# A decoder block on one core: the tensor work of GpSimd moved to the vector engine

## The chip, the cores and the metric

The kernel runs on one core of a Trainium2 chip. The metric is the device time of one execution in microseconds. The median of three runs of the kernel before is 4898.55 us (4892.66 to 4910.54).

## The reference

One layer of a hybrid model for 512 tokens of width 2048, all in float32:

```python
def reference(x, mem, w_in, ..., ln_w, ln_b):
    h = hybrid_mixer(x, ...)                       # mLSTM heads and forgetting attention, gated, merged
    x = layer_norm(DN_ALPHA * x + h, ln_w[l, 0], ln_b[l, 0])
    h = memory_cross_attention(x, mem, ...)        # 256 memory rows
    x = layer_norm(DN_ALPHA * x + h, ln_w[l, 1], ln_b[l, 1])
    h = peer_ffn(x, peer_wq, peer_sub_keys, peer_u, peer_v)
    x = layer_norm(DN_ALPHA * x + h, ln_w[l, 2], ln_b[l, 2])

def peer_ffn(x, w_pq, sub_keys, expert_u, expert_v):
    q = (x @ w_pq).reshape(B, S, 8, 2, 128)
    sc = einsum('bshpd,hpnd->bshpn', q, sub_keys)
    top_s, top_i = lax.top_k(sc, 16)
    cand_s = top_s[..., 0, :, None] + top_s[..., 1, None, :]      # 16 x 16 sums
    best_s, best_pos = lax.top_k(cand_s.reshape(..., 256), 16)
    idx = ...                                      # the expert (of 16384) behind each best sum
    g = jax.nn.softmax(best_s, -1)
    a = einsum('tkd,td->tk', expert_u[idx], x)
    return einsum('tk,tkd->td', gelu(a) * g, expert_v[idx])
```

## The kernel before

**Products in two parts.** TensorE multiplies in a rounded format. To keep float32 accuracy every operand is split: the high part is a copy into the rounded format (ScalarE, L134), the low part is the operand less the high part (a subtraction of a 128x1024 tile, L137 on the vector engine, L136 on GpSimd). Each product is three matmuls: high by high, high by low, low by high. The matmuls with low weights come after those with high ones (`products`, L208).

**Weights** stream from HBM as tiles of 128x1024 (512 KB), in the order of use, loaded by SyncE's queue (`load_raw`, L148) into small rings: `raw`, `whi` and `wlo` have one to three buffers each. A raw buffer can be loaded again when both parts have been made from it. There are 1472 such tiles. Every `SHARE`-th, that is every eighth of those that `load_w` loads up to the end of the choice, has its low part made by GpSimd; during the first 16 tiles of the first mLSTM it is every third. 123 low parts are GpSimd's, 1349 the vector engine's.

**Stages.** The tokens are cut into block A (128) and B (384). First comes A's mixer, with the products of the memory woven into it, up to about 900 us. Then A's merge, cross attention and the query of its experts, woven with B's mLSTM. From about 1460 us, A's experts are gathered row by row (`gathered`): GpSimd issues an indirect load of 128 rows of 2048 (L905), the vector engine multiplies and sums each (L933, L936). Each gather waits for the low part that the vector engine was last given (`work["last"]`), which paces it. Meanwhile B's mixer, cross attention and query run up to about 3080 us. Of B's tokens 96 are gathered too, in two jobs of 64 and 32, and 288 are computed densely over all 16384 experts: `stage_a` (products with `uT`, from 2970 us), and `stage_o` (products with `vq`, from about 3660 us). `stage_o` needs the weights of the choice, which are spread out by one-hot products (L1256, L1262, L1264, about 3360 to 3660 us), written to HBM and read back. 76 chunks of `stage_a` are placed ahead of the first `stage_o`; a chunk is two weight tiles.

**The choice** (`select`) runs for two heads of one block of 128 tokens: top 16 of 128 four times, the 16 x 16 sums `cand` on GpSimd (L832), top 16 of those twice, then for each half of the index a comparison with a counter (L846, vector engine), a product with the indices on GpSimd (L847) and a sum (L848, vector engine). It is called 16 times: four times for A at 1345 to 1500 us, 12 times for B at about 3000 to 3350 us.

**The last norm** (`fin`) is called six times: once for A, once for each of the two gathered parts of B, three times at the very end for the dense tokens. Its first half of 1024 columns takes two vector instructions (L987, L988), its second half one of ScalarE (L990), one product of GpSimd (L991) and one sum of the vector engine (L992).

**Order.** A scheduler lays out each engine's instructions at build time from its own cost estimates, with what the code says as dependences; at run time each engine takes its list in order. GpSimd's list also has the gathers and most of the small transfers to and from HBM.

Of the kernel before, what the change touches and what calls it, by code (L numbers as in the profile page):

```python
# [10 lines left out]
F32 = mybir.dt.float32  # L11
# [4 lines left out]
AF = mybir.ActivationFunctionType  # L16
ALU = mybir.AluOpType
# [14 lines left out]
NDENSE = 288  # L32
GATHERED = ((64, 64), (32, 32))
GB = 48
SHARE = 8
NEG = -1.0e30
ALPHA = 2.0 ** 0.25
EPS = 1e-5
# [8 lines left out]
def build(tc, I, out):  # L47
    nc = tc.nc
    with ExitStack() as ctx:
# [25 lines left out]
        def nm(s):  # L75
            cnt[0] += 1
            return f"{s}_{cnt[0]}"
# [52 lines left out]
        nc.vector.tensor_copy(iota, ioti)  # L130


        def split(hi, lo, src, pool=False):
            nc.scalar.copy(hi, src)  # L134
            if pool:
                return nc.gpsimd.tensor_sub(lo, src, hi.bitcast(F32))  # L136
            return nc.vector.tensor_sub(lo, src, hi.bitcast(F32))  # L137

        def load_split(hi, lo, src):
# [4 lines left out]
        def load_raw(src, n=1024):  # L144
            rings.append(rings.pop(0))
            ring = rings[-1]
            raw = ring["pool"].tile([P, n], F32, tag="raw", bufs=ring["raw"], name=nm("raw"))
            nc.sync.dma_start(raw, src)  # L148
            return raw


        work = {"jobs": None, "rate": 0.0, "due": 0.0, "n": 0, "share": 0, "last": None, "hold": False,
                "quiet": 0, "normed": None}

        def load_pair(src, pool=False):

            raw = load_raw(src)
            ring = rings[-1]
            hi = ring["pool"].tile([P, 1024], F32R, tag="whi", bufs=ring["hi"], name=nm("whi"))
            lo = ring["pool"].tile([P, 1024], F32R, tag="wlo", bufs=ring["lo"], name=nm("wlo"))  # L160
            return hi, lo, split(hi, lo, raw, pool)


        mids = []
# [13 lines left out]
                ride()  # L178

        def load_w(src):  # L180
            work["n"] += 1
            pool = work["share"] and work["n"] % work["share"] == 0
            hi, lo, i = load_pair(src, pool)
            if not pool:
                work["last"] = i
            if work["quiet"]:

                work["quiet"] -= 1
                work["last"] = work["normed"]
            if work["jobs"] is not None and not work["hold"]:  # L190
                work["due"] += work["rate"]
                while work["due"] >= 1 and work["jobs"] is not None:
                    work["due"] -= 1
                    if next(work["jobs"], None) is None:
                        work["jobs"] = None
            return hi, lo
# [52 lines left out]
        def rstd(o, var, t):  # L249

            v, w = t
            nc.vector.tensor_scalar(v, var, EPS, None, op0=ALU.add)
            nc.scalar.activation(w, v, AF.Sqrt)
            nc.vector.reciprocal(w, w)
            nc.vector.tensor_mul(v, v, w)
            nc.vector.tensor_mul(v, v, w)
            nc.vector.tensor_scalar(v, v, -0.5, 1.5, op0=ALU.mult, op1=ALU.add)
            nc.vector.tensor_mul(o, v, w)
# [13 lines left out]
        for kt in range(8):  # L272
            raw = load_raw(I["xT"][kt])
# [8 lines left out]
        def gt(n):  # L282
            return gp.tile([36, S], F32, tag=n, name="g_" + n)

        z, a, e, u, F, gi, M, m = (gt(n) for n in ("z", "a", "e", "u", "F", "gi", "M", "m"))
# [532 lines left out]
        def select(tp, sel, h0, sc, bufs=2):  # L818

            def w(tag, shape, dt=F32):  # L820
                return tp.tile([P] + list(shape), dt, tag=tag, bufs=bufs, name=nm(tag))

            v, ix = w("v", [4, 16]), w("ix", [4, 16], U32)
            for j in range(4):
                top16(tp, sc[:, j * P:(j + 1) * P], P, v[:, j], ix[:, j], bufs)
            ixf = w("ixf", [4, 16])
            nc.vector.tensor_copy(ixf, ix)
            cand = w("cand", [2, 16, 16])
            vv = v.rearrange("p (h q) k -> p h q k", q=2)
            ii = ixf.rearrange("p (h q) k -> p h q k", q=2)  # L830
            full = [P, 2, 16, 16]
            nc.gpsimd.tensor_tensor(cand, vv[:, :, 0].unsqueeze(3).to_broadcast(full),  # L832
                                    vv[:, :, 1].unsqueeze(2).to_broadcast(full), op=ALU.add)
            b, pos = w("b", [2, 16]), w("pos", [2, 16], U32)
            for j in range(2):
                top16(tp, cand[:, j].rearrange("p a b -> p (a b)"), 256, b[:, j], pos[:, j], bufs)
            pi = w("pi", [2, 2, 16], U32)
            nc.vector.tensor_scalar(pi[:, 0], pos, 4, None, op0=ALU.logical_shift_right)
            nc.vector.tensor_scalar(pi[:, 1], pos, 15, None, op0=ALU.bitwise_and)
            pf = w("pf", [2, 2, 16])  # L840
            nc.vector.tensor_copy(pf, pi)
            it = iota[:, 0:16].unsqueeze(1).unsqueeze(1).to_broadcast(full)
            sl = slice(h0 * 16, h0 * 16 + 32)
            for q, m in ((0, "i0"), (1, "i1")):
                eq = w("eq", [2, 16, 16])
                nc.vector.tensor_tensor(eq, pf[:, q].unsqueeze(3).to_broadcast(full), it, op=ALU.is_equal)  # L846
                nc.gpsimd.tensor_mul(eq, eq, ii[:, :, q].unsqueeze(2).to_broadcast(full))  # L847
                nc.vector.tensor_reduce(out=sel[m][:, sl].rearrange("p (h k) -> p h k", h=2), in_=eq,  # L848
                                        axis=AX.X, op=ALU.add)

            nc.vector.tensor_tensor(sel["g"][:, sl].rearrange("p (h k) -> p h k", h=2), b,
                                    b[:, :, 0:1].to_broadcast([P, 2, 16]), op=ALU.subtract)
# [125 lines left out]
        def fin(row, i, acc, lw, n=P):  # L978
            st = fst.pop(i)[:n]
            nc.vector.bn_aggr(st[:, 24:26], st[:, 0:24])  # L980
            rstd(st[:, 26:27], st[:, 25:26], (st[:, 28:29], st[:, 29:30]))
            nc.vector.scalar_tensor_tensor(st[:, 27:28], st[:, 24:25], -1.0, st[:, 26:27], op0=ALU.mult, op1=ALU.mult)
            for q in range(2):
                sl = slice(q * 1024, (q + 1) * 1024)
                a = acc[:n, sl]
                if q == 0:
                    nc.vector.scalar_tensor_tensor(a, a, st[:, 24:25], lw[0][:n, sl], op0=ALU.subtract, op1=ALU.mult)  # L987
                    nc.vector.scalar_tensor_tensor(a, a, st[:, 26:27], lw[1][:n, sl], op0=ALU.mult, op1=ALU.add)  # L988
                else:
                    nc.scalar.activation(a, a, AF.Identity, scale=st[:, 26:27], bias=st[:, 27:28])  # L990
                    nc.gpsimd.tensor_mul(a, a, lw[0][:n, sl])  # L991
                    nc.vector.tensor_add(a, a, lw[1][:n, sl])  # L992
                nc.sync.dma_start(out[row:row + n, sl], a)

        def run(gen):
# [15 lines left out]


        A, B = Path(0, 1, XA), Path(1, 3, XB)
        work["share"] = SHARE
        with tc.tile_pool(name="sa", bufs=1, side="right", reuse_waits="tile") as sa:
            def aq(n=P):
                return sa.tile([P, P], F32, tag="q", bufs=10, name=nm("aq"))
# [25 lines left out]

            with tc.tile_pool(name="a1", bufs=1, side="right", reuse_waits="tile") as a1:
                first = mlstm(A, a1, dict(ka=1, pre=2, qk=6, v=2, o=2, nM=1, pt=2), hold_h)
                work["share"] = 3
                for _ in range(16):
                    next(first)
                work["share"] = SHARE
                pt = sm_bank()  # L1050
                for tb in range(TB):
                    for w, src in enumerate((gi, m)):
                        o = (w * TB + tb) * 4
                        nc.tensor.transpose(pt[:, o:o + 4], src[s4, tb * P:(tb + 1) * P], ident[s4, 32:36])
                nc.vector.tensor_copy(cols.rearrange("p a b c -> p (a b c)"), pt[:, :32])
                gts.close()
                with tc.tile_pool(name="mem", bufs=1, reuse_waits="tile") as mp:
                    mem = memory(mp)
                    weave(chain(first, branch_ml(A, HA, aq)), mem, 0.34)
                    run(mem)  # L1060
                    settle()
# [143 lines left out]
        with tc.tile_pool(name="topk", bufs=1, reuse_waits="tile") as tp:  # L1205
# [22 lines left out]
            for t in range(1, TB - 1):  # L1228
                for g in range(4):
                    select(tp, sel[t], 2 * g, scs[t, g])  # L1230
                soften(tp, sel[t]["g"])
        work["share"] = 0

        def o_bank(i=0):
            return BK["pool"].tile([P, 512], F32, tag="mm", bufs=BK["mm"], name=nm("po"))
# [6 lines left out]
        for hb in range(NDENSE // GB):  # L1242
            while turned * P < (hb + 1) * GB:
                bank = o_bank()
                n = min(P, NDENSE - turned * P)
# [6 lines left out]
            for q in range(GB // 4):  # L1252
# [6 lines left out]
                for u in range(4):  # L1259
# [3 lines left out]
                                            op0=ALU.is_equal, op1=ALU.mult)  # L1263
# [68 lines left out]
        jobs = chain(*(gathered(TB - 1, r0, n, 1 + i, lambda: work["last"], 1) for i, (r0, n) in enumerate(GATHERED)))  # L1332
# [146 lines left out]
```

## Time and profile before

| | |
|---|---|
| median of three runs | 4898.55 us |
| profiled execution | 4901.6 us |
| its span | 4899.9 us |
| mean granted clock of TensorE | 0.985 |
| TensorE busy | 4707.2 us (96%) |
| vector engine busy | 3736.8 us (76%) |
| ScalarE busy | 2130.8 us (43%) |
| GpSimd busy | 1345.5 us (27%) |
| HBM traffic over the span | 292 GB/s |

In the views, PE is TensorE's matmuls and PEld its weight loads, DVE the vector engine, ACT ScalarE, POOL GpSimd, and SP SyncE. A group's row gives line, engine, operation, output and inputs, shapes, and count; behind the first bar busy us and mean ns of one, behind the second the idle time just before and what ended it. A row of waits gives who waited for whom: us in total, times, longest. A busy TensorE is not one at its peak, since matmuls overlap.

### The profile page before, as it was taken

The numbers are of one execution on the slowest core, as the hardware profiler recorded it, in microseconds if no ns is written. First come the engines' busy times: TensorE is split into PE (matmuls) and PEld (weight loads), VectorE is DVE, ScalarE is ACT, GpSimd is POOL, SyncE is SP. The second block draws the span as 40 slices with busy tenths as digits, with TensorE's granted clock in tenths as the row PEclk, the third lists the DMA queues.
The fourth block names the chain that finished last, engine by engine and source line by source line (L and its number), as shares of the span: only waits on it lengthen the run. The fifth ranks groups of instructions, "written<-read, shape, count | busy, mean of one in ns | idle before, by whom it ended". The sixth has DMA issues, their size and how long they took to land. (4 is left out here: it accounts for less than half of the span.)

```text
span 4899.9 us, 75254 instructions
## 1 busy us (share of the span) xinstructions
PE 4707.2 (96%) x28705; PEld 4347.4 (89%) x28705; DVE 3736.8 (76%) x5360; ACT 2130.8 (43%) x3108; POOL 1345.5 (27%) x1058
## 2 busy tenths in 40 slices
PE   7999999999999899999989999999998999999997
PEld 6888778878888899999988779999998999999997
DVE  7776666765698776887768585899877878888886
ACT  6665666555643322343332334434443433343333
POOL 2122222311124444434444232231111222221111
PEclk9999999999999999999999999999999999999999
DMA  7888888866559898998889584588788989989994
GB/s 259 277 290 281 290 321 311 281 226 200 193 188 357 332 358 338 342 334 328 301 297 381 192 298 164 205 281 281 282 290 325 347 339 350 345 332 348 359 336 146
DMA packets 380026, 1433.60 MB, mean 293 GB/s; under 512 B 43852, under 2 KB 104908, under 8 KB 320624
## 3 DMA queue, kind: packets, MB, share of 16 engines
q1 hardware_dynamic: 266208, 831.34, 47.9%
q0 software_dynamic: 91712, 559.45, 30.4%
q10 hardware_dynamic: 21744, 38.02, 2.1%
q8 instruction: 224, 3.67, 0.3%
q14 instruction: 138, 1.13, 0.1%
HBM read 1339.13 MB, written 89.40 MB: 292 GB/s over the span
## 5 line engine op out<-in xcount | busy, mean ns | idle before, releaser
L134 ACT CAST whi<-raw 128x1024 fp32r<-128x1024 f32 x1472 | 1526.1, 1051 | 1769.0 <-PE mm L208 780.0
L137 DVE TENSOR_TENSOR wlo<-raw,whi 128x1024 fp32r<-128x1024 f32 x1349 | 1690.3, 1265 | 711.5 <-ACT whi L134 496.2
L905 POOL DMA_INDIRECT rows<-in_peer_u,eid x224 | 327.4, 1462 | 994.6 <-DVE rows L933 352.0
L905 POOL DMA_INDIRECT rows<-in_peer_v,eid x224 | 367.4, 1640 | 837.6 <-DVE xacc L936 437.1
L208 PE MATMUL po<-hph,whi 128*128 128x288 f32 x2048 | 553.4, 297 | 33.7 <-ACT hph L134 19.5
L933 DVE SCALAR_TENSOR_TENSOR rows<-rows,xacc 128x2048 f32<-128x2048 f32 x224 | 528.0, 2361 | 71.6 <-DMA rows<-in_peer_u,eid 71.1
L936 DVE SCALAR_TENSOR_TENSOR xacc<-rows,dots,xacc 128x2048 f32<-128x2048 f32 x224 | 540.8, 2414 | 42.9 <-DMA rows<-in_peer_v,eid 41.5
L208 PE MATMUL sm<-Ch,whi 128*128 128x288 f32 x2048 | 561.3, 298 | 2.3 <-ACT whi L134 1.3
L208 PE MATMUL sm<-Cl,whi 128*128 128x288 f32 x2048 | 559.1, 297 | 0.0
L208 PE MATMUL po<-hpl,whi 128*128 128x288 f32 x2048 | 553.2, 297 | 1.9 <-DVE hpl L137 1.9
L136 POOL TENSOR_TENSOR wlo<-raw,whi 128x1024 fp32r<-128x1024 f32 x123 | 315.7, 2567 | 714.9 <-ACT whi L134 407.4
L208 PE MATMUL mm<-xh,whi 128*128 128x384 f32 x1280 | 436.7, 343 | 6.5 <-ACT sg L575 2.7
L208 PE MATMUL mm<-xl,whi 128*128 128x384 f32 x1280 | 429.4, 337 | 0.0
L208 PEld LDWEIGHTS po<-hph,whi 128*128 128x128 f32 x2048 | 385.0, 190 | 36.8 <-ACT hph L134 19.7
L208 PEld LDWEIGHTS sm<-Ch,whi 128*128 128x128 f32 x2048 | 385.4, 188 | 4.0 <-ACT whi L134 2.4
L208 PEld LDWEIGHTS po<-hpl,whi 128*128 128x128 f32 x2048 | 385.1, 190 | 3.8 <-DVE hpl L137 2.1
L208 PEld LDWEIGHTS sm<-Cl,whi 128*128 128x128 f32 x2048 | 385.6, 188 | 0.0
L208 PE MATMUL po<-hph,wlo 128*128 128x288 f32 x2048 | 339.3, 296 | 2.0 <-DVE wlo L137 2.0
L208 PE MATMUL sm<-Ch,wlo 128*128 128x288 f32 x2048 | 320.6, 297 | 0.4 <-DVE wlo L137 0.4
L208 PEld LDWEIGHTS po<-hph,wlo 128*128 128x128 f32 x2048 | 295.1, 189 | 5.2 <-DVE wlo L137 3.5
L208 PEld LDWEIGHTS sm<-Ch,wlo 128*128 128x128 f32 x2048 | 287.7, 188 | 2.4 <-DVE hpl L137 0.8
L208 PE MATMUL mm<-xh,wlo 128*128 128x384 f32 x1280 | 255.4, 335 | 0.0
(430 smaller groups left out, 8832.7 us busy)
## 6 DMA issues: line engine op xcount, KB each, us to landing
raw<-in_w_in SPq DMA_DIRECT2D x512, 512.0 KB
raw<-in_uT SPq DMA_DIRECT2D x256, 512.0 KB
raw<-in_vq SPq DMA_DIRECT2D x256, 512.0 KB
raw<-in_w_xkv SPq DMA_DIRECT2D x64, 512.0 KB
raw<-in_w_br_ml SPq DMA_DIRECT2D x64, 512.0 KB
raw<-in_w_br_fx SPq DMA_DIRECT2D x64, 512.0 KB
raw<-in_w_out SPq DMA_DIRECT2D x64, 512.0 KB
raw<-in_peer_wq SPq DMA_DIRECT2D x64, 512.0 KB
```

What stands on the lines that cost most here:

```text
L134: nc.scalar.copy(hi, src)
L136: return nc.gpsimd.tensor_sub(lo, src, hi.bitcast(F32))
L137: return nc.vector.tensor_sub(lo, src, hi.bitcast(F32))
L208: nc.tensor.matmul(o, w if stat else x, x if stat else w, start=k == first and x is xh and not part, stop=k == last and part == 1)
L905: i = nc.gpsimd.indirect_dma_start(out=rows, out_offset=None, in_=I[table], in_offset=bass.IndirectOffsetOnAxis(ap=ei[:, k:k + 1], axis=0))
L933: after(nc.vector.scalar_tensor_tensor(rows, rows, 1.0, xacc, op0=ALU.mult, op1=ALU.mult, accum_out=dots[:, k:k + 1]), last())
L936: after(nc.vector.scalar_tensor_tensor(xacc, rows, dots[:, k:k + 1], xacc, op0=ALU.mult, op1=ALU.add), last())
```

## The change

GpSimd computes no tensors any more. All 1472 low parts, the sums and products of the choice and the whole last norm are made by the vector engine; in the last norm the second half is computed as the first. GpSimd keeps its gathers and small transfers. As each low part is now the vector engine's, `work["last"]` is always that of the last tile. The rest of the code is the same.

```diff
-        def split(hi, lo, src, pool=False):
+        def split(hi, lo, src):
             nc.scalar.copy(hi, src)
-            if pool:
-                return nc.gpsimd.tensor_sub(lo, src, hi.bitcast(F32))
             return nc.vector.tensor_sub(lo, src, hi.bitcast(F32))
...
         def load_w(src):
-            work["n"] += 1
-            pool = work["share"] and work["n"] % work["share"] == 0
-            hi, lo, i = load_pair(src, pool)
-            if not pool:
-                work["last"] = i
+            hi, lo, work["last"] = load_pair(src)
...
-            nc.gpsimd.tensor_tensor(cand, vv[:, :, 0].unsqueeze(3).to_broadcast(full),
+            nc.vector.tensor_tensor(cand, vv[:, :, 0].unsqueeze(3).to_broadcast(full),
                                     vv[:, :, 1].unsqueeze(2).to_broadcast(full), op=ALU.add)
...
-                nc.gpsimd.tensor_mul(eq, eq, ii[:, :, q].unsqueeze(2).to_broadcast(full))
+                nc.vector.tensor_mul(eq, eq, ii[:, :, q].unsqueeze(2).to_broadcast(full))
...
-            nc.vector.scalar_tensor_tensor(st[:, 27:28], st[:, 24:25], -1.0, st[:, 26:27], op0=ALU.mult, op1=ALU.mult)
             for q in range(2):
                 sl = slice(q * 1024, (q + 1) * 1024)
                 a = acc[:n, sl]
-                if q == 0:
-                    nc.vector.scalar_tensor_tensor(a, a, st[:, 24:25], lw[0][:n, sl], op0=ALU.subtract, op1=ALU.mult)
-                    nc.vector.scalar_tensor_tensor(a, a, st[:, 26:27], lw[1][:n, sl], op0=ALU.mult, op1=ALU.add)
-                else:
-                    nc.scalar.activation(a, a, AF.Identity, scale=st[:, 26:27], bias=st[:, 27:28])
-                    nc.gpsimd.tensor_mul(a, a, lw[0][:n, sl])
-                    nc.vector.tensor_add(a, a, lw[1][:n, sl])
+                nc.vector.scalar_tensor_tensor(a, a, st[:, 24:25], lw[0][:n, sl], op0=ALU.subtract, op1=ALU.mult)
+                nc.vector.scalar_tensor_tensor(a, a, st[:, 26:27], lw[1][:n, sl], op0=ALU.mult, op1=ALU.add)
                 nc.sync.dma_start(out[row:row + n, sl], a)
...
-        work["share"] = SHARE
...
-                work["share"] = 3
...
-                work["share"] = SHARE
...
-        work["share"] = 0
```

More of the change, by code (lines that the diff above doesn't have):

```diff
@@ L34 @@
 GB = 48
-SHARE = 8
 NEG = -1.0e30
@@ L149, in load_raw, with load_pair @@
             return raw
-        work = {"jobs": None, "rate": 0.0, "due": 0.0, "n": 0, "share": 0, "last": None, "hold": False,
+        work = {"jobs": None, "rate": 0.0, "due": 0.0, "last": None, "hold": False,
                 "quiet": 0, "normed": None}
-        def load_pair(src, pool=False):
+        def load_pair(src):
             raw = load_raw(src)
@@ L160, in load_pair @@
             lo = ring["pool"].tile([P, 1024], F32R, tag="wlo", bufs=ring["lo"], name=nm("wlo"))
-            return hi, lo, split(hi, lo, raw, pool)
+            return hi, lo, split(hi, lo, raw)
         mids = []
```

## The prediction

> **What bounds the kernel now.** I read the page first (busy shares), then busy time by stages, then the waits of TensorE, then the groups of instructions that the change touches, last the tail. Busy time of TensorE is no measure of its peak, so the second and third views decide.
>
> ```profile
> span 4899.9 us, 75254 instructions
> PE 4707.2 (96%) x28705; PEld 4347.4 (89%) x28705; DVE 3736.8 (76%) x5360; ACT 2130.8 (43%) x3108; POOL 1345.5 (27%) x1058
> ```
>
> TensorE is without an instruction for only 4899.9 - 4707.2 = 192.7 us. By stages (stretch, then busy us of PE, PEld, DVE, ACT, POOL):
>
> ```profile
> 100.00:1300.00 1200.00, 1162.74 (x6271) 992.09 (x6270) 790.94 (x1091) 714.55 (x983) 281.69 (x274) 0.99 0.78 270
> 1300.00:1600.00 300.00, 293.54 (x1417) 247.58 (x1416) 262.27 (x536) 128.00 (x175) 98.65 (x71) 1.00 0.72 262
> ...
> 3100.00:3400.00 300.00, 294.45 (x2215) 293.01 (x2215) 294.87 (x717) 127.83 (x182) 88.12 (x66) 0.99 0.78 268
> 3400.00:3660.00 260.00, 260.00 (x2043) 260.00 (x2042) 221.26 (x419) 125.06 (x349) 24.85 (x18) 1.00 0.79 284
> 3660.00:3700.00 40.00, 20.49 (x142) 20.23 (x141) 18.22 (x29) 9.83 (x20) 3.81 (x2) 0.74 0.82 291
> 3700.00:4800.00 1100.00, 1080.19 (x8021) 1067.90 (x8020) 901.80 (x1014) 420.60 (x532) 245.44 (x157) 1.00 0.91 343
> ```
>
> TensorE is full everywhere but at 3660 us. The vector engine has a third of its time free in the first mixer (790.94 of 1200), little at 1300 to 1600, and nothing at 3100 to 3400 (294.87 of 300), where the choice for the later blocks runs; TensorE has 5.55 us idle there. From 3700 on the change touches only the last norms. What TensorE waits for, where low parts and the high parts ahead of them are concerned:
>
> ```profile
> PE po L208 <- ACT hph L134: 19.5, 1, 19.5
> ...
> PE mm L208 <- ACT whi L134: 9.5, 11, 1.6
> ...
> PE ma L208 <- ACT whi L134: 7.6, 11, 2.0
> ...
> PE ma L208 <- DVE wlo L137: 5.9, 8, 1.5
> PE mm L208 <- DVE wlo L137: 5.6, 7, 2.1
> PE ma L208 <- POOL wlo L136: 5.0, 7, 1.3
> ...
> PE mm L208 <- POOL wlo L136: 1.9, 1, 1.9
> ```
>
> All these waits for low parts together are 18.4 us, 6.9 of them for the 123 that GpSimd makes. The change can win little through them. The one wait of 19.5 us is that at 3660, where the second product over the experts starts.
>
> **The change, part by part.** Moved instructions and their durations (mean in ns behind the bar):
>
> ```profile
> L137 DVE TENSOR_TENSOR wlo<-raw,whi 128x1024 fp32r<-128x1024 f32 x1349 | 1690.3, 1265 | 711.5 <-ACT whi L134 496.2
> ...
> L933 DVE SCALAR_TENSOR_TENSOR rows<-rows,xacc 128x2048 f32<-128x2048 f32 x224 | 528.0, 2361 | 71.6 <-DMA rows<-in_peer_u,eid 71.1
> L936 DVE SCALAR_TENSOR_TENSOR xacc<-rows,dots,xacc 128x2048 f32<-128x2048 f32 x224 | 540.8, 2414 | 42.9 <-DMA rows<-in_peer_v,eid 41.5
> ...
> L136 POOL TENSOR_TENSOR wlo<-raw,whi 128x1024 fp32r<-128x1024 f32 x123 | 315.7, 2567 | 714.9 <-ACT whi L134 407.4
> ```
>
> The same vector instructions with their least, median and greatest ns:
>
> ```profile
> L137 DVE TENSOR_TENSOR wlo<-raw,whi x1349: 1161/1221/3718, 20.3 to 4856.1; 128x1024 fp32r<-128x1024 f32 x193
> ...
> L933 DVE SCALAR_TENSOR_TENSOR rows<-rows,xacc x224: 2267/2285/4822, 1475.8 to 4550.5; 128x2048 f32<-128x2048 f32 x112
> ...
> L936 DVE SCALAR_TENSOR_TENSOR xacc<-rows,dots,xacc x224: 2324/2347/5035, 2119.3 to 4758.6; 128x2048 f32<-128x2048 f32 x112
> ```
>
> and low parts at 3700 to 4300 us, where GpSimd has none:
>
> ```profile
> L137 DVE TENSOR_TENSOR wlo<-raw,whi 128x1024 fp32r<-128x1024 f32 x183 | 219.5, 1221 | 36.1 <-ACT whi L134 34.0 <-issue 2.0
> ```
>
> Added to the vector engine: 123 low parts x 1.221 = 150.2 us. The choice is called 16 times (4 groups in each of 4 blocks) with one sum and two products each: 48 instructions on 128x512. The nearest row is the comparison just ahead of each product, which reads two broadcast operands of that size as they do:
>
> ```profile
> L846 DVE TENSOR_TENSOR eq<-pf,iota 128x512 f32<-128x512 f32 x24 | 15.3, 680 | 0.1
> ```
>
> 48 x 0.680 = 32.6 us. The six last norms gain a 1024-wide instruction each, about 1.2 us: 7 us. Together 190 us.
>
> Given back to it: a low part takes 1.221 us at the median and where GpSimd computes nothing, but 1.265 in the mean and up to 3.718. So the tail of long ones, (1265 - 1221) x 1349 = 59 us, is the price of GpSimd working beside it. In the same way the gathered multiply-adds, (2361 - 2285) x 224 = 17 us, and those of L936, (2414 - 2347) x 224 = 15 us: 91 us, and more in short instructions, which I bound by nothing and another 50 us. The vector engine's net load grows by 50 to 100 us of 3737, to some 78%. A rule of the Trainium skill bears on this row ("SBUF — State Buffer", section "Who interferes with whom"): a vector instruction with two SBUF inputs and a GpSimd one that reads SBUF exclude each other for the whole instruction. By that rule, with each of the 123 blocking half its 2.567 us, 158 us would come back from the low parts alone; the trace shows 59, so the row is taken.
>
> Where does it lie? Off the path, behind a full TensorE, nearly everywhere. Six things can reach the end:
>
> (1) The wait for GpSimd's low parts goes: -6.9 us. What is late next is the vector engine's low part, which would end sooner than GpSimd's by 2.567 - 1.221 = 1.35 us if it starts as early; its waits of 5.9 + 5.6 shrink where they came from lengthened instructions: -3 (bounds 0 and -11.5).
>
> (2) Buffers come free sooner. The loads of raw weights wait for the low part that last read their buffer:
>
> ```profile
> SPq L148 <- DVE wlo L137: 2524.1, 992, 30.2
> SPq L148 <- POOL wlo L136: 394.7, 105, 8.5
> ```
>
> 3.76 us a time behind GpSimd, 2.54 behind the vector engine. An earlier load can shorten the 9.5 + 7.6 = 17.1 us for which TensorE waits for high parts; every eighth is concerned, with its followers: -4 (bounds 0 and -17.1).
>
> (3) Queues. GpSimd's queue loses 123 low parts that waited there with gathers and small transfers behind them; gathers are held by the vector engine's pace anyway. The vector queue takes them in order, behind at most a gathered multiply-add of 2.3 us; TensorE covers that while it has another stream's products: nothing, and +10 where the cover is gone (an estimate: four such waits of 2.4 us).
>
> (4) The stage from 3000 to 3660 us:
>
> ```profile
> L137 DVE TENSOR_TENSOR wlo<-raw,whi 128x1024 fp32r<-128x1024 f32 x108 | 143.8, 1333 | 31.9 <-PE mm L208 30.1 <-ACT whi L134 1.2
> L933 DVE SCALAR_TENSOR_TENSOR rows<-rows,xacc 128x2048 f32<-128x2048 f32 x26 | 64.4, 2476 | 0.4 <-DMA rows<-in_peer_u,eid 0.3
> ```
>
> ```profile
> L847 POOL TENSOR_TENSOR eq<-eq,ixf 128x512 f32<-128x512 f32 x24 | 44.8, 1887 | 69.8 <-DVE eq L846 69.7
> ...
> L832 POOL TENSOR_TENSOR cand<-v 128x512 f32<-128x512 f32 x12 | 15.1, 1260 | 71.4 <-DVE v L815 71.3
> L136 POOL TENSOR_TENSOR wlo<-raw,whi 128x1024 fp32r<-128x1024 f32 x3 | 7.2, 2408 | 15.4 <-PE mm L208 15.4
> ```
>
> Added: 36 x 0.680 + 3 x 1.221 = 28.1 us. Back: (1333 - 1221) x 108 + (2476 - 2285) x 26 = 12.1 + 5.0 = 17.1. Net +11 on a full engine. The order of the changed kernel puts 13 more low parts ahead of the first one-hot tile (1055 against 919 + 123 = 1042), so TensorE has work meanwhile, and the next stretch has 38.7 us of vector time free: +2 (bounds -5 and +28).
>
> (5) The tail:
>
> ```profile
> 4878.15 1.26 DVE L987 SCALAR_TENSOR_TENSOR xr<-xr,fst,lw 128x1024 f32<-128x1024 f32 x1
> ...
> 4882.93 1.27 DVE L988 SCALAR_TENSOR_TENSOR xr<-xr,fst,lw 128x1024 f32<-128x1024 f32 x1
> ...
> 4892.25 4.47 DVE L992 TENSOR_TENSOR xr<-xr,lw 128x1024 f32<-128x1024 f32 x2 [2.24 <-POOL xr L991]
> ```
>
> Now the vector engine ends at 4896.7, having waited for GpSimd's products. After: six subtractions instead of three from 4878.15 (7.6 us), the same small steps (4882.93 - 4878.15 - 3 x 1.26 = 1.0), six multiply-adds (7.6): 4894.4. -2.3.
>
> (6) The scheduler lays out all engines anew; TensorE's products of two streams interleave a little otherwise. Nothing, with 10 us either way (an estimate, about one of the wait rows above).
>
> Sum: -6.9 - 3 - 4 + 0 + 2 - 2.3 + 0 = -14.2. The profiled execution took 4901.6 us (its span and 1.7 around it), so it would take 4887; it lies 3 us over the median of the runs, 4898.55, and the same step from that gives 4884.
>
> **The rivals.** (a) The vector engine becomes the bound at 3100 to 3400 us. "Perfetto Trace Analysis", section "Optimizing Scalar/DVE Operations", of the Trainium skill speaks for it: work may be offloaded from a saturated vector engine even to GpSimd. It adds that the shared port may undo that, and the 3.718 us above agrees. In rows: if the long instructions there are not GpSimd's doing, the 28.1 us come in full to an engine with 5.1 us free and are not made up by 3660, the queue of (3) costs its 10, and of the gains only the tail shows: 28.1 - 5.1 + 10 - 2.3 = +31, so 4929. It decides once TensorE's idle time at 3100 to 3400, 5.55 us, and the 19.5 at 3660 together grow by over 25. Against it: 38.7 us free right after, and the order that moved products ahead.
>
> (b) The port and the buffers were worth more: (1) and (2) at their far bounds, (4) at -5, and the tail: -6.9 - 11.5 - 17.1 - 5 - 2.3 = -43, so 4856. For it: the 3.76 us that a load waits behind GpSimd, and GpSimd's low parts that wait for high parts (its long idle time above) in a queue where other work stands behind them. Against: the vector engine, too, has loads waiting 2.54 us behind it, and will have all of them.
>
> (c) The new order takes it back: the +10 of (3) or of (6) against -14, so 4894 to 4898, no change.
>
> **How the numbers follow.** Forecast 4884 (own range 4870 to 4900): 0.44. (a) 0.22, (b) 0.20, (c) 0.14. A measurement of this kernel can tell about 0.5%, 24.5 us, from no change: faster is below 4874, slower above 4923. Faster: (b) and 0.03 of the forecast, 0.23; slower: (a), 0.22; the rest 0.55. The range runs from a little below (b) to beyond (a), 4850 to 4938, and leaves out some 0.08 on each side.
>
> **What would show it.** Right: the low parts' mean falls to 1.22 us in every stretch; vector busy time rises by 50 to 100 us, not 190; TensorE's waits name no GpSimd; 3100 to 3400 stays full on TensorE; from the first subtraction of the last norms to the last vector instruction it is 16.3 us, not 18.6. Wrong: TensorE idle over 30 us at 3000 to 3700 (a), or the waits for high parts gone (b), or low parts that stay at 1.265.

## The result: 0.66% faster, twice the forecast's step

The changed kernel takes 4867.88 us (median of six runs, 4861.44 to 4869.16), the kernel before in the same comparison 4899.28: 31.4 us less, a ratio of 0.9934 (95% interval 0.992 to 0.9948). The forecast was 4884, with a range of 4850 to 4938. The direction and the range hold; the step was 14 us where 31 came. The time lies 2 us below the forecast's own range (4870 to 4900), 16 from the forecast and 12 from rival (b), and by the prediction's own scale it is "faster" (below 4874), which had a chance of 0.23. The profiled execution of after took 4869.2 us (span 4867.5), 32.4 us under that of before.

The page of after, first the busy shares, then the costliest groups that the change touches:

```profile
span 4867.5 us, 75109 instructions
PE 4697.7 (97%) x28705; PEld 4347.1 (89%) x28705; DVE 3766.3 (77%) x5531; ACT 2127.4 (44%) x3100; POOL 930.7 (19%) x881
...
L134 DVE TENSOR_TENSOR wlo<-raw,whi 128x1024 fp32r<-128x1024 f32 x1472 | 1781.3, 1220 | 711.8 <-ACT whi L133 487.0
...
L929 DVE SCALAR_TENSOR_TENSOR xacc<-rows,dots,xacc 128x2048 f32<-128x2048 f32 x224 | 525.2, 2345 | 24.6 <-DMA rows<-in_peer_v,eid 23.4
...
L926 DVE SCALAR_TENSOR_TENSOR rows<-rows,xacc 128x2048 f32<-128x2048 f32 x224 | 511.2, 2285 | 38.6 <-DMA rows<-in_peer_u,eid 36.6
```

TensorE is without an instruction for 4867.5 - 4697.7 = 169.8 us instead of 192.7, so 22.9 of the 32.4 us are idle time and 9.5 are busy time. The vector engine took on the 190 us that the prediction counted and is busy for only 29.5 us more: some 160 us of lengthening ended. Of those 59 lie in the low parts (123 more of them cost 91.0 us, not 123 x 1.220 = 150.1), 32 in the gathered multiply-adds (528.0 + 540.8 - 511.2 - 525.2), and the other 69 are what is left over for many short instructions.

By stages, the same windows as before (columns: stretch, its length, busy us of PE, PEld, DVE, ACT, POOL, granted clock, DMA share, GB/s):

```profile
100.00:1300.00 1200.00, 1177.51 (x6401) 1011.51 (x6401) 833.47 (x1210) 736.06 (x1021) 118.83 (x212) 0.99 0.81 274
...
3100.00:3400.00 300.00, 297.49 (x2248) 296.78 (x2247) 284.25 (x649) 124.37 (x169) 56.75 (x41) 1.00 0.83 286
3400.00:3660.00 260.00, 240.54 (x1866) 238.88 (x1865) 214.30 (x422) 118.00 (x348) 25.42 (x18) 0.98 0.77 278
3660.00:3700.00 40.00, 36.91 (x259) 36.88 (x260) 27.17 (x38) 16.89 (x28) 6.16 (x4) 0.89 0.86 289
```

The first stretch alone has 15 us more of TensorE's work in it (1177.51 against 1162.74). From 3100 to 3700 TensorE is idle for 2.51 + 19.46 + 3.09 = 25.06 us, and before it was 5.55 + 0 + 19.51 = 25.06 too: the hole ahead of the second expert product came earlier with everything else, and no other took its place.

How far after stands ahead of before at places that both traces have (start or end of a product's records on TensorE; read from the trace; the 2970 us given ahead for `stage_a` is where its weights begin to load):

| place | before, us | after less before, us |
|---|---|---|
| first product of the memory's keys and values | 74.1 | +4.7 |
| last such product | 484.9 | -9.0 |
| last product of A's mixer | 874.5 | -28.4 |
| last product of B's mixer projections | 2863.0 | -28.3 |
| first product of `stage_a` | 3103.8 | -26.6 |
| first product of `stage_o` | 3686.5 | -23.4 |
| last product | 4871.3 | -29.3 |
| end | 4899.9 | -32.4 |

Nearly the whole gain is made before 875 us, in A's mixer woven with the memory's products. There TensorE's waits stand as follows, first before (80 to 899.8 us), then after (80 to 870.4 us, which is the same place in the work):

```profile
PE mm L208 <- ACT whi L134: 7.6, 9, 1.6
PE ma L208 <- ACT whi L134: 6.2, 10, 2.0
PE mm L208 <- ACT mo L392: 4.9, 4, 2.2
PE ma L208 <- POOL wlo L136: 4.3, 6, 1.3
PE sm L371 <- ACT at L366: 3.5, 2, 2.3
PE ma L208 <- ACT o L505: 2.3, 2, 1.8
PE mm L208 <- ACT zo L428: 2.0, 1, 2.0
PE ma L208 <- DVE wlo L137: 1.5, 3, 0.9
```

```profile
PE ma L201 <- ACT whi L133: 4.7, 7, 1.7
PE mm L201 <- ACT whi L133: 3.7, 5, 1.6
PE mm L201 <- ACT mo L385: 1.5, 1, 1.5
PE ma L201 <- ACT o L498: 1.2, 1, 1.2
PE mm L201 <- ACT zo L421: 1.0, 1, 1.0
```

Low parts went from 5.8 us to none, high parts from 13.8 to 8.4. But the waits that name neither (`mo`, `at`, `o`, `zo` and smaller ones) fell too, from 14.7 us to 5.3. A reading of this is that, where one stream stands at such a step, TensorE now more often has another's weights at hand; no run tests it by itself. A second execution of the changed kernel has 5.0 us of such other waits there, and one of choice and norms only, below, where low parts are as before, 13.6. TensorE's busy time to that place fell by 10 us as well, with the granted clock 0.99 before and 1.00 after. The trace of before has four stretches of 3.4 us at half clock there, that of after only the end of one, 5 us long: if a matmul takes twice as long in them, that is 6.8 us lost against 2.5 (an estimate from these lengths). Busy time of this stretch, before and then after:

```profile
80.00:899.80 819.80, 786.31 (x4529) 678.30 (x4530) 547.31 (x682) 511.04 (x714) 207.50 (x201) 0.99 0.85 295
```

```profile
80.00:870.40 790.40, 776.12 (x4544) 676.82 (x4544) 561.97 (x736) 515.48 (x715) 86.19 (x151) 1.00 0.90 307
```

TensorE's weight loads (PEld) have waits of their own. Those for low and high parts in the same two windows, before and then after:

```profile
PEld mm L208 <- ACT whi L134: 13.9, 17, 2.0
PEld ma L208 <- ACT whi L134: 11.6, 14, 2.2
PEld ma L208 <- DVE wlo L137: 7.7, 14, 1.3
PEld ma L208 <- POOL wlo L136: 7.1, 7, 1.8
```

```profile
PEld ma L201 <- ACT whi L133: 8.6, 9, 2.1
PEld mm L201 <- ACT whi L133: 7.7, 11, 2.0
PEld ma L201 <- DVE wlo L134: 3.4, 7, 0.5
```

These fell from 40.3 us to 19.7, and the weight loads' waits for other results from 18.9 to 8.1. Their busy time stayed (678.3 and 676.8 us), so their idle time fell by 27.9 of the 29.4 us. In this account two thirds of the fall bear the name of a low or high part; in the account of the matmuls it was 11.2 us.

### The profile page after: what moved, and what is told of

Its sections match the earlier page's. It is cut to its first block, busy times and chain, and to the rows that moved or that the text cites. A ratio compares the mean times of both kernels' runs of the same rounds, so it can differ in the third digit from the quotient of the medians.

```text
span 4867.5 us, 75109 instructions
## 1 busy us (share of the span) xinstructions
PE 4697.7 (97%) x28705; PEld 4347.1 (89%) x28705; DVE 3766.3 (77%) x5531; ACT 2127.4 (44%) x3100; POOL 930.7 (19%) x881
## 5 line engine op out<-in xcount | busy, mean ns | idle before, releaser
L134 DVE TENSOR_TENSOR wlo<-raw,whi 128x1024 fp32r<-128x1024 f32 x1472 | 1781.3, 1220 | 711.8 <-ACT whi L133 487.0
L201 PE MATMUL po<-hph,whi 128*128 128x288 f32 x2048 | 552.7, 297 | 27.9 <-ACT hph L133 15.8
L929 DVE SCALAR_TENSOR_TENSOR xacc<-rows,dots,xacc 128x2048 f32<-128x2048 f32 x224 | 525.2, 2345 | 24.6 <-DMA rows<-in_peer_v,eid 23.4
L926 DVE SCALAR_TENSOR_TENSOR rows<-rows,xacc 128x2048 f32<-128x2048 f32 x224 | 511.2, 2285 | 38.6 <-DMA rows<-in_peer_u,eid 36.6
L201 PEld LDWEIGHTS mm<-xh,whi 128*128 128x128 f32 x1280 | 241.9, 189 | 14.9 <-ACT whi L133 5.1
```

What stands on the lines that cost most here:

```text
L201: nc.tensor.matmul(o, w if stat else x, x if stat else w, start=k == first and x is xh and not part, stop=k == last and part == 1)
L926: after(nc.vector.scalar_tensor_tensor(rows, rows, 1.0, xacc, op0=ALU.mult, op1=ALU.mult, accum_out=dots[:, k:k + 1]), last())
L929: after(nc.vector.scalar_tensor_tensor(xacc, rows, dots[:, k:k + 1], xacc, op0=ALU.mult, op1=ALU.add), last())
```

## The experiments

Three comparisons, each on one chip with the kernel before beside it (4897.41, 4899.75 and 4898.03 us), so the ratios of one comparison stand on the same runs of before. The changed kernel was compared apart from the first two, 31.4 us under its own before; where a kernel is set against it, the first figure is by the medians, the second by each one's step from its own before.

### Which part: low parts, or choice and norms

**Low parts only** is before with the lines deleted that give GpSimd a share:

```diff
-        work["share"] = SHARE
...
-                work["share"] = 3
...
-                work["share"] = SHARE
```

> The kernel before with only the 123 low parts moved to the vector engine; the choice and the last norms stay on GpSimd. The milestones of the two traces say that some 29 of the 31 us were won before 870 us, where only low parts are moved: about -28 us against before (4871). If the choice and the norms mattered more, -15 or less.

It took 4855.39 us, 0.9906 (0.989 to 0.9923): -42 us, more than the whole change.

**Choice and norms only** is the rest of the change: `select` and `fin` as after, low parts as before.

```diff
-            nc.gpsimd.tensor_tensor(cand, ...)
+            nc.vector.tensor_tensor(cand, ...)
...
-                nc.gpsimd.tensor_mul(eq, eq, ...)
+                nc.vector.tensor_mul(eq, eq, ...)
...
-                    nc.scalar.activation(a, a, AF.Identity, scale=st[:, 26:27], bias=st[:, 27:28])
-                    nc.gpsimd.tensor_mul(a, a, lw[0][:n, sl])
-                    nc.vector.tensor_add(a, a, lw[1][:n, sl])
```

> The kernel before with only the choice's sums and products and the last norms moved; every eighth low part stays on GpSimd. Tail 2 to 3 us shorter, the stage at 3000 to 3660 the same within 5: -3 us against before (4896). The rival that the choice was held up by GpSimd's queue gives -10 or more.

4889.43 us, 0.998 (0.997 to 0.9989): -8 us. The tail explains 2.7 of it. The rest is not the edit's doing: up to the first choice its engines have the same lists as before, and yet its profiled execution was 14.7 us ahead at 875 us (the last product of A's mixer). From there to the first `stage_o` product it loses 11. Its trace has no stretch at half clock from 80 us to that place, where before has the four above, 6.8 us by the estimate there; the rest of the lead stays unexplained. The profiled executions put a bound on such differences. Three have this early order, with GpSimd's low parts (before, this one, and GpSimd early below): they are 0, 14.7 and 2.6 us ahead there. Six have one early order without them (the changed kernel twice, low parts only, GpSimd late, and low parts and norms twice): they are 26.7 to 35.8 ahead (mean 31.7). So the two kinds do not overlap, but a difference of some 10 us in that stretch is not read from a single execution below.

**Low parts and norms**, the choice left on GpSimd, was run in two comparisons, in the second beside the unaltered changed kernel:

> All low parts and the last norms on the vector engine, the choice's sums and products on GpSimd. The tail is 2.3 us shorter than with the low parts alone: 4853. If the choice on the vector engine is what makes the changed kernel slower than the low parts alone (4868 against 4855), this one stays under 4860; if that difference is the spread of single builds, it comes out anywhere between 4853 and 4868.

> The changed kernel once more, beside the next one on the same chip, to tell the choice apart: 4868, 0.6 to 0.7% under before.

> All low parts and the last norms on the vector engine, the choice on GpSimd, once more beside the changed kernel. If the choice's 48 instructions on a full vector engine cost time: 6 to 12 us under the changed kernel. If the earlier difference was spread: within 3 us of it.

4859.16 us, 0.9913 (0.9896 to 0.9929), and again 4858.74 us, 0.992 (0.9904 to 0.9936); the changed kernel beside the second took 4866.3, 0.9926 (0.9911 to 0.9942). The choice on the vector engine looks 8 us dearer, but the intervals overlap. The traces speak for a part of it. From the first product of `stage_a` to the first of `stage_o` the six profiled kernels with the choice on the vector engine take 1.4 to 5.8 us longer than before (mean 3.0), the six with it on GpSimd, half tiles left aside, 0.7 shorter to 1.9 longer (mean 0.2). Half tiles share more tiles in that stage and take 8.8 us longer.

### Where: early or late

GpSimd keeps its low parts only up to the end of A's mixer and the memory's products (`work["share"] = 0` behind them), or only from there on (`work["share"] = SHARE` there, and not before):

> The kernel before, but GpSimd makes low parts only up to the end of the products of the memory (about 890 us); from there on the vector engine makes all. If the gain lies in the first 890 us, as the milestones say, this one stays near the kernel before: 4890 to 4898. If the later stages give part of it: under 4885.

> The mirror of it: the vector engine makes all low parts up to about 890 us, GpSimd every eighth after that; the choice and the norms stay on GpSimd. If the gain lies in the first 890 us: 4855 to 4872, as with all low parts moved (4855). If the later stages give part of it: 4875 to 4885.

GpSimd early: 4892.51 us, 0.9984 (0.9973 to 0.9995). GpSimd late: 4870.42 us, 0.9937 (0.992 to 0.9953). Both leave the choice and the norms on GpSimd, so their measure is low parts only (-42 us), not the changed kernel: of those 42 us the early low parts give back 35 (-7 is left), the late ones 13 (-29 is left). The intervals of GpSimd late and low parts only overlap, and in its trace GpSimd late loses nothing after 875 us (32.2 us ahead there, 34.8 at the end), so a cost of the late ones is not shown. That the low parts of the first 890 us (50 of GpSimd's lie between 80 and 890) are the greater part is. Busy time of the same stretch agrees, first GpSimd early, then GpSimd late:

```profile
80.00:900.00 820.00, 787.45 (x4540) 680.13 (x4541) 546.85 (x685) 512.20 (x713) 208.74 (x202) 0.99 0.85 295
```

```profile
80.00:900.00 820.00, 805.78 (x4707) 704.07 (x4706) 584.73 (x771) 534.46 (x740) 98.12 (x167) 1.00 0.89 307
```

Same length of time, 167 matmuls more, at 307 GB/s instead of 295.

### How: port, held buffer, late low part

The groups of instructions from 80 to 890 us in before, first GpSimd's low parts, then the vector engine's beside them:

```profile
L136 POOL TENSOR_TENSOR wlo<-raw,whi 128x1024 fp32r<-128x1024 f32 x50 | 121.5, 2430 | 322.3 <-ACT whi L134 258.6 <-PE mm L208 48.6 <-PE ma L208 14.7
```

```profile
L137 DVE TENSOR_TENSOR wlo<-raw,whi 128x1024 fp32r<-128x1024 f32 x345 | 443.3, 1303 | 234.6 <-ACT whi L134 202.3 <-PE ma L208 16.1 <-PE mm L208 7.8
```

GpSimd waited for the high part and was then slow; its queue was not what held it. Three things can follow from a slow reader there: it lengthens vector instructions, it holds the raw buffer, and its low part is late. Three kernels take the changed kernel and put one of them back for every eighth tile of that stretch, with GpSimd working on a scratch tile. **Port only:** two subtractions on scratch behind the high part.

```diff
+            if scr is not None and work["n"] % 8 == 0:
+                after_copy(nc.gpsimd.tensor_sub(scr, scr, scr), c)
+                nc.gpsimd.tensor_sub(scr, scr, scr)
```

> The changed kernel, and from about 80 to 890 us, at every eighth weight tile, two subtractions of 128x512 on GpSimd that read and write a scratch tile of their own as soon as the tile's high part is there: GpSimd reads SBUF as long as it did before, but nobody needs what it makes and it holds no weight buffer. Port theory (GpSimd's reading lengthens the vector engine's instructions, and that delays everything): the low parts' mean there rises from 1.22 to about 1.26 us or more, and 20 to 29 of the 29 us come back (4888 to 4897). Theories of the held buffer or of the late low part: at most 5 us come back (4868 to 4873).

The vector engine's low parts in the same stretch of this kernel:

```profile
L165 DVE TENSOR_TENSOR wlo<-raw,whi 128x1024 fp32r<-128x1024 f32 x404 | 533.4, 1343 | 169.2 <-ACT whi L164 151.6 <-PE ma L213 8.6 <-issue 4.7
```

The vector engine's low parts are longer than in before (1343 ns against 1303), and the kernel takes 4870.06 us, 0.994 (0.9924 to 0.9957): 2 to 4 us of the 31, with some 10 either way (an estimate from the two intervals). Lengthened vector instructions are not the main cost.

**Hold only:** four fills of scratch, then a copy of one column of the raw tile, so that the raw buffer comes free late while the low part is made in time.

```diff
+                after_copy(nc.gpsimd.memset(scr, 0.0), c)
+                for _ in range(3):
+                    nc.gpsimd.memset(scr, 0.0)
+                nc.gpsimd.tensor_copy(scr[:, 0:1], raw[:, 0:1])
```

> The changed kernel, and at the same tiles four fills of 128x512 on GpSimd, which read nothing, followed by a copy of one column of the raw tile: the raw buffer is held until GpSimd is through, some 2 us after the high part, while the low part is made by the vector engine in time and the vector engine's instructions are not lengthened (mean 1.22 us). Theory of the held buffer (loads start late, ScalarE and then TensorE wait for them): 15 to 29 us come back (4883 to 4897), and ScalarE's waits for loads of w_in rise again from 69 towards 102 us. Port theory or theory of the late low part: at most 5 us (4868 to 4873).

The same group here, then the waits of SyncE's queue up to 900 us, and those of before:

```profile
L165 DVE TENSOR_TENSOR wlo<-raw,whi 128x1024 fp32r<-128x1024 f32 x407 | 490.9, 1223 | 217.0 <-ACT whi L164 189.3 <-PE ma L215 10.6 <-PE mm L215 8.8
```

```profile
SPq L145 <- POOL scr_m L171: 28.0, 21, 2.4
SPq L145 <- POOL scr_z L171: 24.1, 17, 2.7
```

```profile
SPq L148 <- POOL wlo L136: 106.1, 43, 5.5
```

4878.05 us, 0.996 (0.9946 to 0.9974): 10 to 12 us over the changed kernel, again with some 10 either way, and between the two expectations. Loads do wait for GpSimd (the second fence), 38 times against 43 before, though shorter, 52 us against 106.1. The buffers are not held for less: by the records the copy ends 3.1 us (median) behind the end of a high part, GpSimd's low parts in before 2.5. Why the waits are half as long stays open, so the price may be too low. The sign that was named rises, ScalarE's waits for loads of `w_in` (up to 875 us): 87.1 us against 69.1 in the changed kernel and 101.0 in before. But they are 85.5 in port only, where GpSimd holds no buffer, so it does not tell the two apart.

By their totals, held buffers are some third of the gain and lengthened instructions a tenth. In the stretch itself it is the other way: at 875 us port only is 21.3 us ahead of before and hold only 25.3, against the mean of 31.7 above. Moreover the scheduler laid out all engines anew for these kernels, so each has an early order of its own.

**Late low part:** the same fills, and the vector engine's low part of that tile waits for them.

> The changed kernel, and from about 80 to 890 us, at every eighth weight tile, four fills of 128x512 on GpSimd (they read nothing) after the high part; the vector engine makes that tile's low part only after them. The low part comes some 2 us later and its raw buffer is held, as with GpSimd's own low parts, but no vector instruction is lengthened. Theory of the late low part: 20 to 29 us come back (4888 to 4897), at least 10 more than with the buffer held alone (4878). If late low parts cost nothing beyond the held buffer: 4873 to 4882. Port theory: at most 5 us over the changed kernel (4868 to 4873).

The vector engine's waits for GpSimd up to 900 us:

```profile
DVE wlo L170 <- POOL scr_z L169: 26.5, 12, 5.4
...
DVE wlo L170 <- POOL scr_m L169: 16.2, 9, 3.1
```

4912.65 us, 1.0024 (1.0014 to 1.0034), 44 to 45 us over the changed kernel and 13 over before. It overshoots, and the rows suggest why: the vector engine itself stood for 43 us in these waits, with the next low parts behind it, which GpSimd's own queue never did to it. It does not measure the price of lateness.

**Half tiles** is before with every fourth tile shared instead of every eighth, and only its second half given to GpSimd, so that GpSimd's share should end with the vector engine's; `work["last"]` is now that of every tile, since the vector engine has a part in each:

```diff
-                return nc.gpsimd.tensor_sub(lo, src, hi.bitcast(F32))
+                nc.gpsimd.tensor_sub(lo[:, 512:], src[:, 512:], hi.bitcast(F32)[:, 512:])
+                return nc.vector.tensor_sub(lo[:, :512], src[:, :512], hi.bitcast(F32)[:, :512])
```

> The kernel before, but GpSimd makes half of the low part (512 columns) of every fourth tile instead of all of every eighth (every second of the first 16 instead of every third), and the vector engine the other half at the same time. GpSimd subtracts as much as before, lengthens vector instructions as much, and its queue is as long; but such a low part is ready after about 1.3 us instead of 2.57. Theory of the late low part: most of the 29 us is won, 4865 to 4880. If GpSimd's work itself, its queue or the port is the cause: 4890 to 4900, as before.

The two halves from 80 to 890 us, GpSimd's and the vector engine's:

```profile
L136 POOL TENSOR_TENSOR wlo<-raw,whi 128x512 fp32r<-128x512 f32 x101 | 161.0, 1594 | 388.6 <-ACT whi L134 314.2 <-PE ma L208 32.7 <-PE mm L208 26.1
```

```profile
L137 DVE TENSOR_TENSOR wlo<-raw,whi 128x512 fp32r<-128x512 f32 x101 | 101.7, 1006 | 47.8 <-ACT whi L134 37.2 <-PE mm L208 6.1 <-PE ma L208 2.0
```

4891.59 us, 0.9984 (0.9973 to 0.9995): by its time this is the answer of the rival, that GpSimd's work itself costs and not its lateness. The trace is less plain. The halves slow each other (1006 ns for 512 columns, when 1024 take 1220 undisturbed), so by the records these tiles are done 1.9 us (median) behind the end of a high part, against 2.5 for GpSimd's whole tiles before and 1.3 for low parts in the changed kernel. And the profiled execution was 23.9 us ahead at 875 us, most of the gain, but only 10.6 at the first `stage_o` product: it lost later more than half of what it had won, perhaps through its twice as many shared tiles. The expectation was about the total and missed; the stage speaks for lateness, from one execution and with an order of its own.

### A version better than both

**First tiles on GpSimd** takes the better kernel (choice on GpSimd) and gives GpSimd every third of the first 16 tiles, to win back the +4.7 us at 74 us (a second execution of the changed kernel stands at +1.9 there):

> As the one before (choice on GpSimd), and GpSimd also makes every third low part of the first 16 tiles, where the changed kernel's first memory product came 4.7 us later than in the kernel before. If the vector engine is short at the start: 3 to 5 us under the one before. If the 4.7 us came from the order alone or the late low parts cost the same there: within 3 us or slower.

4861.79 us, 0.9928 (0.9912 to 0.9944), against 4858.74 without it: nothing won. Low parts all on the vector engine and the choice on GpSimd, with the norms on either, remains the fastest (0.9906, 0.9913 and 0.992, whose intervals overlap).

## Why the prediction was right, and too small

Its direction rested on a full TensorE with a vector engine that has room, and that held. The wide range held thanks to the rivals that it spans; the size did not. Of the signs named, the low parts' mean (1212 to 1223 ns in every stretch), no wait of TensorE for GpSimd, a full TensorE from 3100 to 3400 us (297.49 of 300) and the tail came; the rise of vector busy time did not. Step by step:

- **Vector load.** Forecast +50 to +100 us, came +29.5. The rowed part was exact (59 and 32 us back, forecast 59 and 17 + 15). The bound of 50 for short instructions was too low; 69 came back there. By the rule of the Trainium skill ("SBUF — State Buffer", section "Who interferes with whom") and the prediction's half of each of GpSimd's subtractions, the low parts alone would have given back 158 us (an estimate); they gave 59. Whether a GpSimd instruction blocks for less, or the vector engine often stood idle beside it, no run here shows.
- **(1) Waits for low parts**, -6.9 and -3. TensorE's rows for them on the two banks `mm` and `ma` fell from 18.4 us to 6.6, in size as forecast. TensorE's waits after, over the whole span:

```profile
PE mm L201 <- ACT whi L133: 13.5, 9, 4.8
...
PE ma L201 <- ACT whi L133: 5.5, 8, 1.7
PE mm L201 <- DVE wlo L134: 4.0, 5, 1.9
PE ma L201 <- DVE wlo L134: 2.6, 2, 2.3
```

- **(2) Buffers**, -4 by the waits for high parts. Over the whole span these did not fall at all (13.5 + 5.5 against 17.1): 5.4 us went in the first 870 us and came back in single waits elsewhere (4.0 us at the start, 4.8 us in B's stages). The size came from another row than the cost: hold only shows some 10 us.
- **The step that failed** is the sum's form. (1) and (2) were counted on the matmuls' waits that name low and high parts. In the stage that matters those fell by 5.8 + 5.4 = 11.2 us, while the stretch became 29.4 us shorter. Another 9.4 us were waits that name other results, and 10.2 us were TensorE's busy time (waits and idle time differ by 1.4 us, so the three come to 30.8). The prediction had no term for these two. The weight loads' waits, which it did not use, name low and high parts for 20.6 us of the fall, so the parts were under-counted as well. It saw that GpSimd's low parts wait long for high parts, and priced that in rival (b) alone.
- **(3) Queues**, nothing: the whole gain remained at 2863 us (-28.3 after -28.4), though the gathers run between. Right.
- **(4) The stage from 3000 to 3660 us**, +2 (-5 to +28): +3.2 from the first `stage_a` to the first `stage_o` product. The size was right; that the products put ahead were the cover is not tested.
- **(5) The tail**, -2.3: the table's last two rows give -3.1. From the first subtraction to the last vector instruction it takes 4864.39 - 4848.85 = 15.54 us, forecast 16.3 (the vector engine's timeline at the end; start and length):

```profile
4848.85 2.46 DVE L978 SCALAR_TENSOR_TENSOR xr<-xr,fst,lw 128x1024 f32<-128x1024 f32 x2
...
4857.14 7.25 DVE L979 SCALAR_TENSOR_TENSOR xr<-xr,fst,lw 128x1024 f32<-128x1024 f32 x6
```

**The rivals.** (a) needed 25 us more of idle time from 3100 to 3700; there was none. The rule it drew on, to offload a saturated vector engine ("Perfetto Trace Analysis", section "Optimizing Scalar/DVE Operations", of the Trainium skill), holds in a small way: the choice on GpSimd leaves that stage 3 us shorter, while the page's caution about the shared port fits the 160 us that came back. (b), 4856, had the right place, buffers and low parts, and is nearer in size than the forecast was (12 us off against 16), though the far bound of its waits for high parts was not what gave it. (c) is excluded by the interval.

**Settled and open.** Shown: the gain is the low parts', the greater part of it in the first 870 us; by totals, lengthened vector instructions alone take back 2 to 4 us of it and held buffers alone 10 to 12, each with some 10 either way, so neither is the whole. That the rest, some 15 to 19 us, is the late low part itself, which leaves the other stream without cover, is argued from the waits and from the half tiles' first stage; late low part overshoots, half tiles miss in the total, hold only and port only change places in the stretch itself, and so the split is not settled. One rival was not tested: all kernels without GpSimd's early low parts also have another order of instructions from the start, and no run changes one without the other. Part of the gain may be that of the order, which the prediction's step (6) held for 10 us either way.

## What to carry to other kernels

A helper's cost on a full engine is not the sum of the matmuls' waits that bear its name: the weight loads' waits were twice as large here, and waits that name other results fell with them. Price such a change by stage, from the rate at which the full engine's work goes through, and find the stage by giving the helper its work early only and late only. Keep a slow helper off the tiles that feed the full engine. What stands on the vector engine where that one is saturated it may have: here the choice on GpSimd was 3 us shorter in its stage, and 8 by medians whose intervals overlap.

## What the hardware showed that was not expected

Fills by GpSimd, which read nothing, lengthened no vector instruction: low parts 1223 ns beside 200 fills of 128x512 in the stretch, 1343 ns beside 100 subtractions of the same size. And one group of small vector instructions was lengthened far more for its size than the low parts (3.7% in the mean, 1265 against 1220 ns): the convolution's multiply-adds on 128x128, before and after:

```profile
L490 DVE SCALAR_TENSOR_TENSOR qk<-pre,c_conv_w,qk 128x128 f32<-128x128 f32 x48 | 21.7, 476 | 0.2
```

```profile
L483 DVE SCALAR_TENSOR_TENSOR qk<-pre,c_conv_w,qk 128x128 f32<-128x128 f32 x48 | 15.3, 345 | 0.2
```

That is 38% in the mean. GpSimd early has 433 ns for this group, GpSimd late 347.
